# A hybrid decoder layer on one core: the conv state's share moved into FFN 1, ten taps per tile made by TensorE with diagonal matrices

## The chip, the core and the metric

The kernel runs on one NeuronCore of one Trainium2 chip. The metric is the device time of one execution in microseconds, the median of three runs. An execution uses five engines with a queue each: TensorE (PE; PEld are its weight loads), VectorE (DVE), ScalarE (ACT), GpSimd (POOL) and SyncE (SP), which issues the DMAs. Each engine works its own list of instructions strictly in order and waits where a semaphore tells it to.

## What is computed

One layer: half an FFN, a mixer, half an FFN. There are 256 prompt tokens and 64 decoded ones (8 sequences of 8), so T = 320 columns everywhere. The model width is 2048, an FFN 5632. The mixer has 16 attention heads and, beside them, 1024 channels of a convolution over time, 31 taps wide, each channel for itself:

```python
a, b = jnp.split(c, 2, axis=-1)
u = a * jax.nn.sigmoid(b)
...
u_ext = jnp.pad(u, ((0, 0), (CONV_STATE, 0), (0, 0)))                    # prompt: zeros ahead
conv = conv_branch(u_ext, dw_w, dw_b, ln_g, ln_b)
...
u_ext = jnp.concatenate([state_conv[l].astype(u.dtype), u], axis=1)      # decoded: 30 old values ahead
conv = conv_branch(u_ext, dw_w, dw_b, ln_g, ln_b)
...
def conv_branch(u_ext, dw_w, dw_b, ln_g, ln_b):
    y = lax.conv_general_dilated(u_ext, dw_w[:, None, :], window_strides=(1,), padding='VALID', ...)
    return jax.nn.silu(layernorm(y + dw_b, ln_g, ln_b))
```

For a decoded token the sum over 31 taps so falls into a share of the state, which is an input, and a share of the at most eight new values of its sequence. The layer norm goes over all 1024 channels. The attention of the decoded tokens reads a cache of 2048 positions (here called the sample work), that of the prompt tokens is small.

## The kernel before

**Layout.** Activations lie transposed, channels on the 128 partitions and T = 320 tokens along them: 16 tiles `yT` for the width, 8 tiles `cacc` for the conv's channels.

**Weights.** A weight piece is loaded by SP (`raw`), rounded by ACT to a high part `wh` (L243), and DVE makes the rest `wl` (L244); PE multiplies three times (L312 to L314: high by high, high by low, low by high) with 320 columns each. In FFN 1 and FFN 2 a piece is 4 x 128 rows by 256 columns, 24 products, and `wh` and `wl` have three buffers. In the mixer (`feed`, L743 and on) a piece is 2 x 128 by 256, 12 products; LA = 3 pieces are loaded ahead, LS = 1 piece is split ahead.

**The mixer's order.** First the q and k columns of w_in, then conv columns four times (`conv_in`: a gemm for a, one for b, two tiles each, 64 pieces in all), then the v columns four times (32 pieces), then W_out, its conv half first. After every piece `gemm` calls `tick()`, which runs what was put off with `defer(n, ...)`, and `after()`, which is `pump(na, nb)`: it advances the sample work by `na` steps, with a higher priority, and takes `nb` steps off a queue `bg` of background work. A scheduler then moves instructions within each engine by these priorities and an estimated timeline; what results is one fixed list for each engine.

**The sample work.** Per decoded sequence there are six far steps (POOL multiplies 128x1024 keys by the query, L569, DVE reduces them, L570; buffers `kf`, three of them), four near steps (keys are transposed by PE, `misc_kt` L593, and multiplied, `S` L600) and ten value steps (L659, L667).

**The convolution** (`conv_taps`). When a tile's b columns are there, `ev_b` loads its state (`state_in`: a DMA, two PE transposes, an ACT copy), POOL makes u (L844) and ACT copies it into a buffer of three, beside the state. Then `bg` gets the tile's steps. 21 taps are DVE's (L767 the first, L769). Ten taps (PTAPS) are ACT's and POOL's: ACT scales u (`cprod`, L774), POOL adds it up (`csum`, L778). Two steps `stap` make the decoded tokens: POOL multiplies 31-wide windows of state and new values by the taps (128x992, into a `kf` buffer, L787), DVE reduces them (L789). A last step adds `csum` (L802) and sums the tile for the norm. NBG = 5 steps go per piece. After the last conv tile come the 18 steps of the conv norm (`conv_norm`: mean, eight subtractions with squares, variance, eight scalings with SiLU). What is left in `bg` after the v columns runs at once.

Of the kernel before, what the change touches and what calls it, by code (L numbers as in the profile page):

```python
# [48 lines left out]
RATE_K = 0.55  # L49
RATE = 1.05  # L50
RATE_O = 1.6
NBG = 5
ORDER = "ccccvvvv"
MERGE = "fnffnfvnfvfvnvvvvvvv"
UW = ST + SEQ
UB = ST + TD
UTOT = UW + NB * UB
STG0, STGN = 16, 256


# [50 lines left out]
def block(ctx, tc, A, O):  # L111
# [105 lines left out]
    def tables():  # L217
# [81 lines left out]
    def gemm(feed, nk, hi, lo, evac, after=None, before=None):  # L299

        acc = [acc_tile() for _ in range(2)]
        for pc in range(nk // feed.nkp):
            if before:
                before(pc, feed)
            wh, wl = feed.get()
            for j in range(2):
                for k in range(feed.nkp):
                    kk = feed.nkp * pc + k
                    st, sp = kk == 0, kk == nk - 1
                    a = acc[j][:, 0:T]  # L310
                    h, l = wh[:, k, P * j:P * j + P], wl[:, k, P * j:P * j + P]
                    nc.tensor.matmul(a, h, hi[kk], start=st, stop=False)  # L312
                    nc.tensor.matmul(a, h, lo[kk], start=False, stop=False)  # L313
                    nc.tensor.matmul(a, l, hi[kk], start=False, stop=sp)  # L314
            tick()
            if after:
                after()
        for j in range(2):
            evac(j, acc[j][:, 0:T])

    class Ffn:
        def __init__(self, name, side=None):
# [104 lines left out]

        return f

    f1.run(W("ffn1_w_gate"), W("ffn1_w_up"), W("ffn1_w_down"), n1, lambda g: (nm.feed(g), nm.feed(g + 1)), x_chunks)  # L430


    mix = ExitStack()
# [315 lines left out]
    cprod = deque(cp.tile([P, 384], F32, name=f"cprod{i}", bufs=1) for i in range(3))
    csum = deque(cp.tile([P, 384], F32, name=f"csum{i}", bufs=1) for i in range(2))  # L750
    srow = deque(cp.tile([120, 2, P], F32, name=f"srow{i}", bufs=1) for i in range(2))
    ubuf = deque(cp.tile([P, UTOT], F32, name=f"u{i}", bufs=1) for i in range(3))
    for u in ubuf:
        nc.gpsimd.memset(u[:, 0:ST], 0.0)
    stf = A["state_conv"][0].rearrange("b t c -> (b t) c")
    ncp = O["new_conv_prompt"][0, 0]
    ncs = O["new_conv_sample"][0][:, ST - TD:ST, :]

    def conv_taps(i, u):
        a = cacc[i]  # L760
        ap, bias = a[:, 0:SEQ], gains[:, DWB + i:DWB + i + 1]
        s2 = {}

        def tap(j):
            w, src = dww[:, i, j:j + 1], u[:, j:j + SEQ]
            if j == 0:
                nc.vector.tensor_scalar(ap, src, w, bias, op0=ALU.mult, op1=ALU.add)  # L767
            else:
                nc.vector.scalar_tensor_tensor(ap, src, w, ap, op0=ALU.mult, op1=ALU.add)  # L769

        def ptap(j):
            first = "c" not in s2
            t = turn(csum if first else cprod)[:, 0:SEQ]
# [19 lines left out]
        nd = CW - PTAPS
        for j in range(nd):
            bg.append(lambda j=j: tap(j))
            k = (j + 1) * PTAPS // nd - j * PTAPS // nd
            for x in range(k):
                bg.append(lambda x=j * PTAPS // nd + x: ptap(nd + x))
            if j in (3, 9):
                bg.append(lambda j=j: stap(j > 3))  # L800
        def close():
# [15 lines left out]
    def state_in(i):  # L817
        sr = turn(srow)
        nc.sync.dma_start(sr, stf[:, P * i:P * i + P].rearrange("(r p) c -> p r c", p=120))
        m = mtile("st")  # L820
        for r in range(2):
            nc.tensor.transpose(m[:, 120 * r:120 * r + 120], sr[:, r, :], ident[0:120, 0:120])
        u = turn(ubuf)
        nc.scalar.copy(u[:, UW:UTOT].rearrange("p (b t) -> p b t", t=UB)[:, :, 0:ST],
                       m[:, 0:240].rearrange("p (b t) -> p b t", t=ST))
        return u

    def conv_in(g, after):
        at = {}
# [6 lines left out]
        def ev_b(j, ps):  # L836
            i = g + j
            t = wt("bt")
            nc.vector.tensor_tensor(t, ps, rstd, op=ALU.mult)
            nc.scalar.activation(t, t, AF.Sigmoid)  # L840
            u = state_in(i)
            us = u[:, UW:UTOT].rearrange("p (b t) -> p b t", t=UB)
            uc = at[j]
            nc.gpsimd.tensor_tensor(uc, at[j], t, op=ALU.mult)  # L844
            nc.scalar.copy(u[:, ST:UW], uc[:, 0:SEQ])
            nc.scalar.copy(us[:, :, ST:UB], uc[:, SEQ:T].rearrange("p (b t) -> p b t", t=TD))
            defer(6, lambda: u_out(i, uc))
            conv_taps(i, u)

# [222 lines left out]
```

## Time and profile before

| what | us |
|---|---|
| median of three runs | 2631.21 (2628.18 to 2635.72) |
| the profiled execution | 2634.91 |
| its span, first to last instruction | 2633.1 |
| PE busy | 2523.2 (96%) |
| DVE busy | 1458.9 (55%) |
| ACT busy | 1031.6 (39%) |
| POOL busy | 436.4 (17%) |

Busy shares are means over stages with different limits, so the slices of the span and windows of it are what to read. Times in the trace are counted from the span's start. A recorded matmul lasts longer than its turn in the array, since products are pipelined; PE's true rate is read from starts. PEclk is the share of the full clock (2.4 GHz) that TensorE was granted.

### The profile page before, as it was taken

To read this page: it belongs to the slowest core of one execution; us is meant where nothing else is said; L and a number is where in the kernel's file an instruction comes from. 1 tells how busy PE (TensorE), PEld (TensorE's weight loads), DVE (VectorE), ACT (ScalarE), POOL (GpSimd) and SP (SyncE) were. 2 spreads that over 40 slices of the span, in tenths; PEclk is the share of its full clock that TensorE was granted. 3 is DMA by queue.
4 is the path that set the end of the run, shared out by engine and by line. 5 is a ranking of instruction groups with operands and counts; after the bars stand their busy time and mean duration, and the time that the engine had idled before them with its cause. 6 is when DMAs were issued, how large, how long until landed. Compare 5 with 4: busy or idle time off the path is not lost.

```text
span 2633.1 us, 43093 instructions
## 1 busy us (share of the span) xinstructions
PE 2523.2 (96%) x17516; PEld 2411.1 (92%) x17516; DVE 1458.9 (55%) x1785; ACT 1031.6 (39%) x1605; POOL 436.4 (17%) x384
## 2 busy tenths in 40 slices
PE   8999999999999999798777899999999999999999
PEld 7999999999999999677666676999999999999999
DVE  5444444444444577969999744644444444444443
ACT  5332333233333456455443444533333333333333
POOL 2000000000000124737666300200000000000000
PEclk9999999999999999899988899999999999999999
DMA  7766767767667655776667756444444444444443
GB/s 221 214 205 212 205 214 208 210 212 203 213 216 199 203 158 180 219 220 211 223 217 250 235 178 212 133 150 152 147 150 153 148 149 152 149 148 152 151 148 119
DMA packets 486263, 489.60 MB, mean 186 GB/s; under 512 B 118250, under 2 KB 463266, under 8 KB 485280
## 3 DMA queue, kind: packets, MB, share of 16 engines
q1 hardware_dynamic: 486064, 486.84, 59.5%
q8 instruction: 137, 2.24, 0.4%
q14 instruction: 62, 0.51, 0.1%
HBM read 478.78 MB, written 59.04 MB: 204 GB/s over the span
## 4 chain that ended last, share of the span: by engine, by line
PE 41%; DVE 7%; issue 6%; DMA 2%; POOL 1%; ACT 1%; SPq 0%; ACTq 0%; DVEq 0%; POOLq 0%
PE acc L314 13%; PE acc L312 13%; PE acc L313 13%; DVE cacc L769 3%; DVE wl L244 2%; PE S L667 0%; DVE sf L570 0%; PE misc_kt L593 0%; DMA kf<-farK 0%; DMA raw<-w_out 0%; POOL kf L569 0%; PE S L600 0%; DVE cacc L892 0%; DVE cacc L767 0%; DMA kn<-cache_k 0%
## 5 line engine op out<-in xcount | busy, mean ns | idle before, releaser
L244 DVE TENSOR_TENSOR wl<-raw,wh 128x1024 fp32r<-128x1024 f32 (+1 forms) x736 | 871.6, 1186 | 923.4 <-ACT wh L243 920.1
L243 ACT CAST wh<-raw 128x1024 fp32r<-128x1024 f32 (+1 forms) x736 | 687.7, 936 | 1252.5 <-PE acc L313 1110.4
L314 PE MATMUL acc<-xh_a,wl 128*128 128x320 f32 x1408 | 436.1, 310 | 0.0
L313 PE MATMUL acc<-xl_a,wh 128*128 128x320 f32 x1408 | 436.1, 310 | 0.0
L312 PE MATMUL acc<-xh_a,wh 128*128 128x320 f32 x1408 | 435.5, 310 | 0.2 <-ACT wh L243 0.2
L314 PE MATMUL acc<-hh,wl 128*128 128x320 f32 x1408 | 435.5, 309 | 0.0
L312 PE MATMUL acc<-xh_c,wh 128*128 128x320 f32 x1408 | 435.3, 309 | 0.0
L314 PE MATMUL acc<-xh_c,wl 128*128 128x320 f32 x1408 | 435.1, 309 | 0.0
L313 PE MATMUL acc<-xl_c,wh 128*128 128x320 f32 x1408 | 435.1, 309 | 0.0
L313 PE MATMUL acc<-hl,wh 128*128 128x320 f32 x1408 | 435.0, 309 | 0.0
L312 PE MATMUL acc<-hh,wh 128*128 128x320 f32 x1408 | 435.0, 309 | 0.0
L368 POOL TENSOR_TENSOR hm<-ut,sg 128x320 f32<-128x320 f32 x88 | 78.4, 891 | 1652.9 <-DVE ut L366 1652.0
L314 PE MATMUL acc<-xh_b,wl 128*128 128x320 f32 x640 | 208.2, 341 | 67.1 <-DVE wl L244 66.9
L312 PEld LDWEIGHTS acc<-xh_a,wh 128*128 128x128 f32 x1408 | 264.8, 188 | 1.1 <-ACT wh L243 0.6
L314 PEld LDWEIGHTS acc<-xh_a,wl 128*128 128x128 f32 x1408 | 264.9, 188 | 0.5 <-issue 0.2
L313 PEld LDWEIGHTS acc<-xl_a,wh 128*128 128x128 f32 x1408 | 265.0, 188 | 0.3
L313 PEld LDWEIGHTS acc<-xl_c,wh 128*128 128x128 f32 x1408 | 264.3, 188 | 0.1
L312 PEld LDWEIGHTS acc<-xh_c,wh 128*128 128x128 f32 x1408 | 264.3, 188 | 0.1
L313 PEld LDWEIGHTS acc<-hl,wh 128*128 128x128 f32 x1408 | 264.3, 188 | 0.0
L314 PEld LDWEIGHTS acc<-hh,wl 128*128 128x128 f32 x1408 | 264.3, 188 | 0.0
L314 PEld LDWEIGHTS acc<-xh_c,wl 128*128 128x128 f32 x1408 | 264.3, 188 | 0.0
L312 PEld LDWEIGHTS acc<-hh,wh 128*128 128x128 f32 x1408 | 264.1, 188 | 0.0
(212 smaller groups left out, 2985.6 us busy)
## 6 DMA issues: line engine op xcount, KB each, us to landing
raw<-ffn_w_gate SPq DMA_DIRECT2D x176, 512.0 KB, 3.6
raw<-ffn_w_up SPq DMA_DIRECT2D x176, 512.0 KB, 3.8
raw<-ffn_w_down SPq DMA_DIRECT2D x176, 512.0 KB, 3.5
raw<-w_in SPq DMA_DIRECT2D x128, 256.0 KB, 4.1
farK<-cache_k SPq DMA_DIRECT2D x64, 384.0 KB, 4.8
farV<-cache_v SPq DMA_DIRECT2D x48, 512.0 KB, 4.8
kf<-farK SPq DMA_DIRECT2D x48, 512.0 KB, 4.6
vn<-farV SPq DMA_DIRECT2D x48, 512.0 KB, 5.7
```

Of the source, the lines that this page charges most:

```text
L243: nc.scalar.copy(dsth, src)
L244: nc.vector.tensor_tensor(dstl, src, dsth.bitcast(F32), op=ALU.subtract)
L312: nc.tensor.matmul(a, h, hi[kk], start=st, stop=False)
L313: nc.tensor.matmul(a, h, lo[kk], start=False, stop=False)
L314: nc.tensor.matmul(a, l, hi[kk], start=False, stop=sp)
L368: nc.gpsimd.tensor_tensor(m, t, sg[j], op=ALU.mult)
L769: nc.vector.scalar_tensor_tensor(ap, src, w, ap, op0=ALU.mult, op1=ALU.add)
```

## The change

- The state's share of the decoded tokens, with the bias, is made in FFN 1. `state_part` puts off one load per tile (`defer(40 + 20 * i)`), PE transposes, ACT copies the state into windows padded with zeros for the new values, and for each of 8 sequences DVE multiplies a 128x248 window by the taps and reduces it into `cold`. A table `wz` holds the taps that meet new values.
- In the mixer `stap` is one step: DVE multiplies the new values by `wz` (128x512), reduces, and adds `cold`.
- The ten ACT and POOL taps go. `diag` makes ten 128x128 diagonal matrices per tile on ACT, `dtaps` has PE multiply them with u in f32 and sum them in PSUM, and DVE's evacuation adds the bias. The 21 taps of DVE follow.
- u is written by POOL at its place at once, in one of five buffers; two ACT copies go. A tile may wait in the program for a buffer, by running `bg` steps.
- NBG is 2.6 steps per piece, with a carried rest.

```diff
-NBG = 5
+NBG = 2.6
...
+        for t in range(TD):
+            nc.gpsimd.tensor_copy(wz[:, :, t, 0:t + 1], dww[:, :, CW - 1 - t:CW])
...
+    def state_part(pool, win):
+        def load(i):
+            sr = pool.tile([120, 2, P], F32, name="srow", bufs=1)
+            nc.sync.dma_start(sr, stf[:, P * i:P * i + P].rearrange("(r p) c -> p r c", p=120))
+            defer(8, lambda: work(i, sr))
+
+        def work(i, sr):
+            m = mtile("st")
+            for r in range(2):
+                nc.tensor.transpose(m[:, 120 * r:120 * r + 120], sr[:, r, :], ident[0:120, 0:120])
+            o = win
+            nc.scalar.copy(o.rearrange("p (b t) -> p b t", t=UB)[:, :, 0:ST],
+                           m[:, 0:240].rearrange("p (b t) -> p b t", t=ST))
+            w = dww[:, i, :][:, None, :].to_broadcast([P, TD, CW])
+            for b in range(NB):
...
+                pr = pool.tile([P, TD, CW], F32, name="spr", bufs=1)
+                nc.vector.tensor_tensor(pr, x, w, op=ALU.mult)
+                nc.vector.tensor_reduce(cold[:, i, TD * b:TD * b + TD], pr, axis=mybir.AxisListType.X, op=ALU.add)
+            nc.scalar.activation(cold[:, i, :], cold[:, i, :], AF.Identity, bias=gains[:, DWB + i:DWB + i + 1])
+
+        for i in range(8):
+            defer(40 + 20 * i, lambda i=i: load(i))
...
     def bg_run(n):
-        while n > 0 and bg:
+        bgc[0] += n
+        while bgc[0] >= 1 and bg:
             bg.popleft()()
-            n -= 1
+            bgc[0] -= 1
...
+            for x in range(PTAPS // 2 * h, PTAPS // 2 * (h + 1)):
+                nc.scalar.activation(dg[0][:, x, :], ident, AF.Copy, bias=0.0, scale=dww[:, i, nd + x:nd + x + 1])
+
+        def dtaps():
+            m = mtile("dt")
+            for x in range(PTAPS):
+                nc.tensor.matmul(m[:, 0:SEQ], dg[0][:, x, :], u[:, nd + x:nd + x + SEQ], start=x == 0,
+                                 stop=x == PTAPS - 1)
+            nc.vector.tensor_scalar(ap, m[:, 0:SEQ], bias, None, op0=ALU.add)
...
-            nc.scalar.activation(t, u[:, j:j + SEQ], AF.Copy, bias=0.0, scale=dww[:, i, j:j + 1])
...
-                nc.gpsimd.tensor_tensor(s2["c"], s2["c"], t, op=ALU.add)
...
-            nc.gpsimd.tensor_tensor(pr4, win, w, op=ALU.mult)
...
-            nc.vector.tensor_reduce(d, pr.rearrange("p (b j) -> p b j", j=CW), axis=mybir.AxisListType.X, op=ALU.add)
...
+            nc.vector.tensor_tensor(pr, x, wz[:, i, :, :][:, None, :, :].to_broadcast([P, NB, TD, TD]), op=ALU.mult)
...
+            nc.vector.tensor_reduce(d, pr.rearrange("p b t s -> p (b t) s"), axis=mybir.AxisListType.X, op=ALU.add)
+            nc.vector.tensor_tensor(d, d, cold[:, i, :], op=ALU.add)
+
+        bg.extend([lambda: diag(0), lambda: diag(1), stap, dtaps])
+        bg.extend([lambda j=j: tap(j) for j in range(nd)])
+        bg.append(lambda: (norm_add("m", a, i), ran.append(i)))
...
-            nc.gpsimd.tensor_tensor(ap, ap, s2["c"], op=ALU.add)
...
+            while len(ran) < i - len(ubuf) + 1:
+                bg.popleft()()
+            u = turn(ubuf)
+            uc = u[:, ST:UT]
             nc.gpsimd.tensor_tensor(uc, at[j], t, op=ALU.mult)
-            nc.scalar.copy(u[:, ST:UW], uc[:, 0:SEQ])
```

Three places show how the lists of the engines change. The first is DVE in FFN 1, in a pair of gate and up columns; `gt` and `ut` are the evacuations. Before:

```order
L244 TENSOR_TENSOR wl<-raw,wh 128x1024 x3
L359 TENSOR_TENSOR gt<-acc,rstd 128x320 x2
L244 TENSOR_TENSOR wl<-raw,wh 128x1024 x4
L366 TENSOR_TENSOR ut<-acc,rstd 128x320 x2
L244 TENSOR_TENSOR wl<-raw,wh 128x1024
```

After, where the last conv tile's state is worked off:

```order
L391 TENSOR_TENSOR gt<-acc,rstd 128x320 x2
L248 TENSOR_TENSOR wl<-raw,wh 128x1024
L346 TENSOR_TENSOR spr<-win,dww 128x248
L347 TENSOR_REDUCE cold<-spr 128x8
...
L346 TENSOR_TENSOR spr<-win,dww 128x248
L248 TENSOR_TENSOR wl<-raw,wh 128x1024
L347 TENSOR_REDUCE cold<-spr 128x8
```

Two to three pairs of product and reduction now stand between two `wl`, eight pairs for a tile, eight tiles.

The second is DVE among the conv columns of the mixer, where a tile's taps begin. Before (tiles 9338 and 9339 are the fifth and the sixth):

```order
L767 TENSOR_SCALAR cacc_9338<-u_11053,dww,gains 128x256
L769 SCALAR_TENSOR_TENSOR cacc_9338<-u_11053,dww,cacc_9338 128x256 x4
L244 TENSOR_TENSOR wl<-raw,wh 128x512
L767 TENSOR_SCALAR cacc_9339<-u_11051,dww,gains 128x256
L769 SCALAR_TENSOR_TENSOR cacc_9338<-u_11053,dww,cacc_9338 128x256
L769 SCALAR_TENSOR_TENSOR cacc_9339<-u_11051,dww,cacc_9339 128x256
L244 TENSOR_TENSOR wl<-raw,wh 128x512
```

After (9601 is the third tile, 9602 the fourth, `nm` the norm's sum, `sf` a far step's reduction):

```order
L878 TENSOR_TENSOR nm_12265<-nm_12265,cacc_9601 128x320
L606 TENSOR_REDUCE sf<-kf 128x16
L655 RECIPROCAL st<-st 128x1
L816 TENSOR_SCALAR cacc_9602<-misc_dt,gains 128x256
L819 SCALAR_TENSOR_TENSOR cacc_9602<-u_11313,dww,cacc_9602 128x256
L606 TENSOR_REDUCE sf<-kf 128x16
L819 SCALAR_TENSOR_TENSOR cacc_9602<-u_11313,dww,cacc_9602 128x256 x2
L606 TENSOR_REDUCE sf<-kf 128x16
L819 SCALAR_TENSOR_TENSOR cacc_9602<-u_11313,dww,cacc_9602 128x256
L248 TENSOR_TENSOR wl<-raw,wh 128x512
```

Two tiles' taps were interleaved; now one tile is done after the other, and each begins with an evacuation of PE's sum `misc_dt`.

The third is PE around the mean of the conv norm (`misc_mu`). Before, among v columns (`xh_b`, `xl_b`):

```order
L312 MATMUL acc<-xh_b_9153,wh 128x320
L313 MATMUL acc<-xl_b_9154,wh 128x320
L868 MATMUL misc_mu<-nm_11916,onesC 128x320
L659 MATMUL misc_pt<-ident,px 128x128 x4
L314 MATMUL acc<-xh_b_9153,wl 128x320
```

After, with the last v transposes (`misc_vo`) ahead and the first conv product of W_out (`ch`) at the end:

```order
L922 MATMUL misc_vo<-ident,w_9622 128x128 x2
L923 MATMUL misc_vo<-ident,w_9622 64x128
L883 MATMUL misc_mu<-nm_12265,onesC 128x320
L883 MATMUL misc_mu<-nm_12652,onesC 128x320
L883 MATMUL misc_mu<-nv_14963,onesC 128x320
L695 MATMUL misc_pt<-ident,px 128x128 x4
L667 MATMUL misc_pl<-vS,ptz 32x256 x4
L883 MATMUL misc_mu<-nv_14968,onesC 128x320
L703 MATMUL S<-vn,pt 32x256 x12
...
L316 MATMUL acc<-ch_15017,wh 128x320 x2
```

The mean and the variance moved from the middle of the v columns to behind them, with a few value blocks of the sample work between them and W_out.

## Rows read from the trace of the kernel before

**Rows 1.** The page's 40 slices of the span, busy tenths, and clock tenths

```profile
PE   8999999999999999798777899999999999999999
DVE  5444444444444577969999744644444444444443
PEclk9999999999999999899988899999999999999999
```

**Rows 2.** Busy time by stretch: FFN 1, the mixer's stage, W_out

```profile
core 0: us, PE busy (x) PEld busy (x) DVE busy (x) ACT busy (x) POOL busy (x), PEclk, DMA share, GB/s
300.00:900.00 600.00, 600.00 (x4093) 600.00 (x4093) 269.53 (x294) 203.13 (x230) 26.69 (x31) 1.00 0.70 210
1118.60:1482.00 363.40, 294.81 (x2305) 242.77 (x2304) 334.86 (x402) 181.12 (x404) 216.49 (x170) 0.91 0.69 226
1482.00:1640.00 158.00, 148.03 (x1136) 106.50 (x1136) 76.53 (x226) 62.64 (x168) 9.09 (x8) 0.96 0.59 195
```

**Rows 3.** Waits from 1118 to 1482: who, for whom, us, times, longest

```profile
PE acc L314 <- DVE wl L244: 54.9, 32, 5.0
```

**Rows 4.** DVE's groups, 1118 to 1482: busy us, mean ns, idle before

```profile
L769 DVE SCALAR_TENSOR_TENSOR cacc<-u,dww,cacc 128x256 f32<-128x256 f32 x160 | 137.4, 890 | 0.5
L244 DVE TENSOR_TENSOR wl<-raw,wh 128x512 fp32r<-128x512 f32 x94 | 96.0, 1025 | 16.6 <-ACT wh L243 16.6
L570 DVE TENSOR_REDUCE sf<-kf 128x16 f32<-128x1024 f32 x29 | 34.9, 1205 | 0.0
L789 DVE TENSOR_REDUCE cacc<-kf 128x32 f32<-128x992 f32 x16 | 18.8, 1174 | 0.0
L892 DVE TENSOR_TENSOR cacc<-cacc,mu 128x320 f32<-128x320 f32 x4 | 7.1, 1804 | 0.0
L767 DVE TENSOR_SCALAR cacc<-u,dww,gains 128x256 f32<-128x256 f32 x8 | 7.0, 880 | 4.5 <-ACT u L845 4.5
L879 DVE TENSOR_TENSOR cacc<-cacc,mu 128x320 f32<-128x320 f32 x8 | 7.0, 945 | 0.8 <-ACT mu L876 0.8
```

**Rows 5.** POOL's groups, 1118 to 1482

```profile
L569 POOL TENSOR_TENSOR kf<-kf,qr 128x1024 f32<-128x1024 f32 x28 | 71.4, 2552 | 24.0 <-DMA kf<-farK 16.6 <-DVE cacc L769 6.4 <-DVE st L619 1.0
L778 POOL TENSOR_TENSOR csum<-csum,cprod 128x256 f32<-128x256 f32 x72 | 65.0, 906 | 12.1 <-ACT cprod L774 9.1
L787 POOL TENSOR_TENSOR kf<-u,dww 128x992 f32<-128x992 f32 x16 | 38.6, 2420 | 14.7 <-DVE cacc L789 6.5 <-ACT u L824 5.3 <-DVE sf L570 2.7
...
L802 POOL TENSOR_TENSOR cacc<-cacc,csum 128x256 f32<-128x256 f32 x8 | 8.0, 1002 | 18.2 <-DVE cacc L769 18.2
```

**Rows 6.** DVE's timeline: start us, length of the run us, instruction, count

```profile
1209.38 3.60 DVE L769 SCALAR_TENSOR_TENSOR cacc<-u,dww,cacc 128x256 f32<-128x256 f32 x4
1212.90 1.22 DVE L244 TENSOR_TENSOR wl<-raw,wh 128x512 fp32r<-128x512 f32 x1
1214.05 4.92 DVE L769 SCALAR_TENSOR_TENSOR cacc<-u,dww,cacc 128x256 f32<-128x256 f32 x11
1218.89 0.68 DVE L244 TENSOR_TENSOR wl<-raw,wh 128x512 fp32r<-128x512 f32 x1
```

**Rows 7.** PE's timeline: one f32 product with 320 columns (two records)

```profile
1454.14 0.70 PE L868 MATMUL misc_mu<-nv,onesC 128*128 128x320 f32 x2
1454.68 0.38 PE L907 MATMUL misc_vo<-ident,w 128*128 128x128 f32 x2
```

**Rows 8.** PE's value products, 1118 to 1482 (eight records a block)

```profile
L667 PE MATMUL S<-vn,pt 128*32 128x256 f32 x400 | 34.7, 416 | 3.1 <-DMA vn<-farV 2.8 <-ACT pt L553 0.3
```

**Rows 9.** Timeline of the conv norm: mean, reciprocal, first W_out product

```profile
1434.92 0.81 PE L868 MATMUL misc_mu<-nm,onesC 128*128 128x320 f32 x2
...
1458.04 2.15 DVE L889 RECIPROCAL mu<-sd 128x320 f32<-128x320 f32 x1 [1.47 <-ACT sd L887]
...
1481.86 0.39 PE L312 MATMUL acc<-ch,wh 128*128 128x320 f32 x1
```

**Rows 10.** DVE's groups, 300 to 900: the weights' rest in FFN 1

```profile
L244 DVE TENSOR_TENSOR wl<-raw,wh 128x1024 fp32r<-128x1024 f32 x171 | 216.5, 1266 | 288.0 <-ACT wh L243 288.0
```

More of the change, by code (lines that the diff above doesn't have):

```diff
@@ L51 @@
 RATE_O = 1.6
-NBG = 5
+NBG = 2.6
 ORDER = "ccccvvvv"
 MERGE = "fnffnfvnfvfvnvvvvvvv"
-UW = ST + SEQ
+UT = ST + T
 UB = ST + TD
-UTOT = UW + NB * UB
 STG0, STGN = 16, 256
@@ L141, in block @@
     dww = const.tile([P, 8, CW], F32, name="dww")
+    wz = const.tile([P, 8, TD, TD], F32, name="wz")
+    nc.gpsimd.memset(wz, 0.0)
+    cold = const.tile([P, 8, TS], F32, name="cold")
     G1, GM, G2, DWB, LNG, LNB, QN, KN = 0, 16, 32, 48, 56, 64, 72, 73
@@ L428, in x_chunks @@
         return f
-    f1.run(W("ffn1_w_gate"), W("ffn1_w_up"), W("ffn1_w_down"), n1, lambda g: (nm.feed(g), nm.feed(g + 1)), x_chunks)
+    with tc.tile_pool(name="stp", bufs=1) as stp:
+        win = stp.tile([P, NB * UB], F32, name="win")
+        nc.gpsimd.memset(win, 0.0)
+        state_part(stp, win)
+        f1.run(W("ffn1_w_gate"), W("ffn1_w_up"), W("ffn1_w_down"), n1, lambda g: (nm.feed(g), nm.feed(g + 1)), x_chunks)
     mix = ExitStack()
@@ L705, in block @@
     bg = deque()
+    bgc = [0.0]
     def bg_run(n):
-        while n > 0 and bg:
+        bgc[0] += n
+        while bgc[0] >= 1 and bg:
             bg.popleft()()
-            n -= 1
+            bgc[0] -= 1
+        if not bg:
+            bgc[0] = 0.0
     smp = sample()
@@ L748, in block @@
     cp = cst.enter_context(tc.tile_pool(name="cp", bufs=2))
[L749 to L752, printed above, removed]
+    ubuf = deque(cp.tile([P, UT], F32, name=f"u{i}", bufs=1) for i in range(5))
     for u in ubuf:
         nc.gpsimd.memset(u[:, 0:ST], 0.0)
-    stf = A["state_conv"][0].rearrange("b t c -> (b t) c")
     ncp = O["new_conv_prompt"][0, 0]
     ncs = O["new_conv_sample"][0][:, ST - TD:ST, :]
+    ran = []
     def conv_taps(i, u):
@@ L761, in conv_taps @@
         ap, bias = a[:, 0:SEQ], gains[:, DWB + i:DWB + i + 1]
-        s2 = {}
-        def tap(j):
[L765 to L773, printed above, removed]
-            nc.scalar.activation(t, u[:, j:j + SEQ], AF.Copy, bias=0.0, scale=dww[:, i, j:j + 1])
-            if first:
-                s2["c"] = t
-            else:
-                nc.gpsimd.tensor_tensor(s2["c"], s2["c"], t, op=ALU.add)
@@ L793, in conv_taps @@
[L793 to L801, printed above, removed]
-            nc.gpsimd.tensor_tensor(ap, ap, s2["c"], op=ALU.add)
-            norm_add("m", a, i)
-        bg.append(close)
+        nd = CW - PTAPS
@@ new lines, in conv_taps, with diag @@
+        dg = []
+        def diag(h):
+            if not dg:
+                dg.append(cp.tile([P, PTAPS, P], F32, name="diag"))
+            for x in range(PTAPS // 2 * h, PTAPS // 2 * (h + 1)):
[6 more added lines that the diff above has]
+            nc.vector.tensor_scalar(ap, m[:, 0:SEQ], bias, None, op0=ALU.add)
@@ new lines, in tap, with stap @@
+        def tap(j):
+            nc.vector.scalar_tensor_tensor(ap, u[:, j:j + SEQ], dww[:, i, j:j + 1], ap, op0=ALU.mult, op1=ALU.add)
+        def stap():
+            pr = cp.tile([P, NB, TD, TD], F32, name="cpr", bufs=1)
+            x = u[:, ST + SEQ:UT].rearrange("p (b s) -> p b s", b=NB)[:, :, None, :].to_broadcast([P, NB, TD, TD])
+            nc.vector.tensor_tensor(pr, x, wz[:, i, :, :][:, None, :, :].to_broadcast([P, NB, TD, TD]), op=ALU.mult)
+            d = a[:, SEQ:T]
+            nc.vector.tensor_reduce(d, pr.rearrange("p b t s -> p (b t) s"), axis=mybir.AxisListType.X, op=ALU.add)
+            nc.vector.tensor_tensor(d, d, cold[:, i, :], op=ALU.add)
@@ L815, in u_out @@
         nc.sync.dma_start(ncs[:, :, P * i:P * i + P], uo[0:TS, 1, :])
[L817 to L826, printed above, removed]
     def conv_in(g, after):
```

16 lines of the change are left out of this document (3 added, 13 removed).

## The prediction

> **What bounds the kernel now.** I read the page's slices first [rows 1]. TensorE (PE) is at 9 tenths nearly everywhere, except in slices 15 to 22, the mixer. There VectorE (DVE) climbs to 9 and PE's granted clock drops from full. The busy times by stretch [rows 2] say the same in numbers. In FFN 1 (300 to 900 us) PE is busy 600 of 600 us and DVE 270. From the end of the k columns to the first W_out product (1118.6 to 1482, which I call the stage: 363.4 us for the conv and v columns) DVE is busy 334.9 us, PE 294.8 at a clock of 0.91. After it (1482 to 1640) PE is busy 148 of 158 us, and DVE has half its time free. So FFN 1 and FFN 2 are PE's, the stage is DVE's. The waits confirm it [rows 3]: PE stood 54.9 us before the third product of a weight piece, 32 times, until DVE had made `wl`. The code makes only one piece ahead (LS = 1), so every tap that DVE has queued before the next `wl` is time for PE too.
>
> Why is DVE so long in it? Its groups [rows 4]: 160 taps of 890 ns, 137.4 us, and 94 `wl` of 1025 ns, 96.0 us. Neither needs that long. At 1214 us eleven taps take 4.92 us together, 0.45 each, and the `wl` behind them 0.68; 5 us earlier four taps take 3.60, 0.90 each, and the `wl` next to them 1.22 [rows 6]. What differs is GpSimd (POOL): in the stage it is busy 216.5 us [rows 2] with products of two tensors [rows 5]. The reductions, with one input, last 1174 to 1205 ns on the whole stage [rows 4], so they are not slowed. The Trainium skill, "SBUF — State Buffer", section "Who interferes with whom", gives the rule: a VectorE instruction with two SBUF inputs and a GpSimd instruction that reads SBUF exclude each other for a whole instruction. The trace agrees: 0.45 against 0.90 us, and reductions that don't change.
>
> **The change, part by part.** I make the sum against the profiled run (2634.91 us, span 2633.1; median of the runs 2631.21) and apply the difference to the median.
>
> *POOL work that goes.* 72 additions of `csum` (65.0 us), 16 state products (38.6) and 8 closing additions (8.0) [rows 5] make 111.6 us, 52% of POOL's 216.5. DVE's time lost to POOL is 160 x (0.89 - 0.45) = 70 us in taps and 94 x (1.025 - 0.64) = 36 in `wl` (0.64: the recorded 0.68 less some of the 0.08 by which records overlap, as the eleven taps' end at 1218.97 and the `wl` behind them show [rows 6]). Of these 106 I give back 52%: 55 us. Below lies 40, if the far multiplications (28 of 2552 ns [rows 5]) hold DVE more once POOL is free for them; above 106. By the page's rule alone, each of the 111.6 us could be 1 us of DVE back, and DVE's sum below would be 198 and not 255.
>
> *DVE instructions.* Gone: 16 state reductions, 18.8 us [rows 4]. Each tile had 1 + 20 taps and now has 21 taps and one evacuation of the diagonal products, some 0.45 more, which the contended first taps (7.0 us for 8 [rows 4]) pay for: 0. New: for each of 8 tiles a product over 512 elements (0.64, like a `wl`), a reduction over 512 (1.17 x 512/992 = 0.6) and a small addition (0.2): 11.5. In the order of after, 32 far reductions stand between the last k column and W_out, where the trace of before has 29 [rows 4]: 3 x (1.2 + 1.6) = 8. DVE: 334.9 - 55 - 18.8 + 11.5 + 8 = 281. Of it about 26 (subtractions and scalings of the conv norm, 7.0 + 7.1 [rows 4], with their additions, splits and the reciprocal) now stands behind all v columns. That leaves **DVE 255 us** for conv and v columns.
>
> *PE.* Ten products with a diagonal in f32, 128x256, for each of 8 tiles: the nearest row is the mean's product, f32, 320 columns, 0.54 us until the next starts [rows 7]. By columns 0.43, x 80 = 34 us. The bound above: if each of its two weight loads were not hidden, 30 us more. The 16 state transposes go to FFN 1: -2. In the order of after, PE has also done 8 more value blocks and 2 more key blocks at the first W_out product. 50 value blocks (400 records) took 34.7 us [rows 8], so 8 take 5.6; I count 6 in all, and take 6 off behind the stage, where PE is the bound. What PE does now is 294.8 us at clock 0.91 [rows 2], or 268 at full clock. **PE: 268 + 34 - 2 + 6 = 306 us**, more than DVE's 255. So the bound changes engines, and conv and v columns take 306. Here the clock decides. In FFN 1, where PE never stops, the clock is 1.00; in the stage, where it waits for `wl`, 0.91 [rows 2], a mix of the levels 1.2 and 2.4 GHz. The Trainium skill, "TensorE: Matmul & The Clock Gate", section "What's actually happening", says that an idle array gets the slow clock and a busy one the full. By that rule 306; with the clock of now 295 + 34 - 2 + 6 = 333. FFN 1 agrees, so I take 306.
>
> *The conv norm.* NBG goes from 5 to 2.6 per weight piece while a tile still has 26 background steps (34 before). 8 x 26 + 18 are 226 steps, 80 pieces x 2.6 only 208: the 18 of the norm run after the last v column. The order says so too: PE's mean product stands behind the last v transposes. Now the norm takes from 1434.92 (second mean product) to 1481.86 (first W_out product) [rows 9], but PE has v columns and DVE other work in between. Alone it is two mean products (1.1), 8 subtractions (3.6 at 0.45), squares and sums on ACT, POOL and DVE (3), two variance products (1.1), root and its table (2), the reciprocal (2.15 [rows 9]), scaling, SiLU and split of the first tile (2), with copies and signals: some 18 us. PE finds only a few value blocks in it, and then the tiles arrive slower than it eats them. I charge **+18** (bounds 8, and 47, the length now).
>
> *FFN 1.* 64 pairs of product and reduction over 248 elements go onto DVE: 0.45 + 0.35 (estimates from the tap and from 1.17 x 248/992), 51 us in all. Three pairs between two `wl` are 2.4 + 1.27 = 3.7 us; a weight piece costs PE 24 x 600/4093 = 3.5 [rows 2]. DVE sat idle 288 us before its 171 `wl` [rows 10], and pieces are three buffers deep, so a burst of two pieces is hidden. If that cover were gone: 51 us. PE pays for the 16 transposes, 2. Eight small loads on the SP queue stand among pieces that it issues ahead. I charge **+4** (2 to 12): 2 for the transposes, 2 for what bursts leave.
>
> *The sum.* Stage 363 -> 306 + 18 = 324: -39. Behind it -6. FFN 1 +4. Total -41: 2594 for the profiled run, **2590** for the median.
>
> **Rivals.**
>
> *The engines alternate.* An evacuation of the diagonal products stands in DVE's order with less than a piece of `wl` made ahead, so DVE waits there for PE, and then PE for the `wl` that stands some ten rows further on: 8 x 4.3 us of products that overlap nothing, or PE stays at 0.91. Conv and v columns 333 to 340: 2617 to 2624. For it: the one-piece lead, and PE's 32 waits now [rows 3]. Against: PE has key and value blocks in between.
>
> *PE has more room than its rows tell.* A weight product lasts 0.31 us in its record and the next starts after 0.15, so every burst ends with time that isn't needed. Then conv and v columns take about 280, near DVE's 255: 2564.
>
> *Weight loads of the diagonals aren't hidden:* +30, 2620. Against: the mean's two passes follow each other in 0.54 us, loads included [rows 7].
>
> *Slower: DVE's new work in FFN 1 is not hidden.* All 64 pairs delay `wl` and with it PE. If half of the products meet POOL's `hm` as taps meet `csum`, a pair is 0.68 + 0.35, 64 of them 66 us in place of the 2 charged for bursts' rest: 2654. It decides once DVE's lead over PE is under one burst's excess over its pieces, some 2 x 1 us. Against: 288 idle us before `wl` [rows 10], PE without a pause there, POOL busy only 27 of 600 us [rows 2].
>
> **How the numbers follow.** Forecast 0.55 (2575 to 2612), more room 0.17, alternation 0.17, loads 0.04, FFN 1 not hidden 0.07. From the first three comes the range, 2558 to 2626; it leaves out little more than FFN 1. A measurement tells 0.3%, 7.9 us: faster is below 2623.3, slower above 2639.1. Faster: 0.55 + 0.17 + half of alternation and of loads = 0.82; same 0.11; slower 0.07.
>
> **What the profile after would show.** Taps near 0.6 us in place of 0.89 and `wl` near 0.8; PE over 90% busy from the k columns to the mean product at a clock near 1, its wait for `wl` well under 30 us; 160 records of diagonal products with 0.21 us spacing; a gap of 10 to 18 us in PE after the last v column; in FFN 1 no wait of PE for `wl`. I would be wrong if taps kept their 0.89, if PE's wait for `wl` stayed (alternation), or if FFN 1 grew by over 10 us.

## The result, and the profile after

The changed kernel takes **2600.97 us** (median, 2596.43 to 2607.19); the kernel before took 2633.14 beside it. The ratio is 0.9882, 95% interval 0.9851 to 0.9912: 32 us faster, where 41 were forecast. The profiled execution (2597.02, near the low end of its runs) has a span of 2595.2 us against 2633.1, so the traces show 37.9 us of difference.

The page's slices of after, to be read against [rows 1]: DVE's nines went from five to two, PE's sevens in slices 19 to 21 (counted from 0) are nines, and the clock has one eight left. Slice 17 (1103 to 1168 us, the end of the k columns and the first conv columns) fell from nine to seven.

```profile
PE   8999999999999999879999899999999999999999
DVE  5445555555544477987897646644444444444443
PEclk9999999999999999899999999999999999999999
```

For the mixer I cut the windows at DVE's last evacuation of the k, of the conv and of the v columns, and at the first product of each half of W_out. Columns as in [rows 2]. Before (conv columns, v columns, W_out's conv half):

```profile
1118.70:1350.60 231.90, 192.35 (x1550) 159.37 (x1548) 207.46 (x262) 120.53 (x266) 132.22 (x112) 0.93 0.66 215
1350.60:1480.60 130.00, 100.97 (x737) 82.30 (x737) 125.90 (x141) 59.18 (x136) 82.87 (x58) 0.87 0.73 244
1481.90:1633.80 151.90, 141.93 (x1101) 101.45 (x1099) 73.00 (x216) 57.87 (x156) 9.19 (x8) 0.96 0.58 191
```

After (FFN 1, conv columns, v columns, the gap up to W_out, its conv half):

```profile
300.00:900.00 600.00, 600.00 (x4096) 599.97 (x4095) 305.10 (x390) 206.74 (x242) 26.39 (x30) 1.00 0.69 211
1119.80:1351.90 232.10, 210.67 (x1696) 174.17 (x1695) 187.18 (x268) 109.86 (x253) 90.71 (x58) 0.96 0.80 263
1351.90:1449.60 97.70, 97.39 (x825) 85.89 (x823) 72.09 (x134) 42.40 (x98) 15.28 (x13) 1.00 0.73 239
1449.60:1471.10 21.50, 12.26 (x81) 5.88 (x81) 13.92 (x22) 12.71 (x26) 7.51 (x8) 0.76 0.55 182
1471.10:1595.90 124.80, 123.86 (x944) 91.95 (x944) 64.53 (x212) 57.75 (x154) 3.32 (x4) 1.00 0.52 175
```

The surprise is in the lengths. The conv columns, where 82 of the 111.6 us of removed POOL work had stood, are as long as before: 232.1 and 231.9. The v columns lose 32.3 us, the gap costs 20.2 more, and W_out's conv half loses 27.1. What follows lasts 999.3 us in both.

A second reading makes this comparable, and I use it for every kernel below. Busy time of PE times its granted clock is PE's **work at full clock**; what the window has beyond that is **lost** (PE waits, or runs slowly). It is an estimate, since the granted clock is the mean of a window and has two digits: a hundredth of it is 2 us in the conv columns. From the last k evacuation to W_out's second half:

| kernel | conv | v | gap | W_out conv half | work | lost |
|---|---|---|---|---|---|---|
| before | 231.9 | 130.0 | 1.3 | 151.9 | 404 | 111 |
| after | 232.1 | 97.7 | 21.5 | 124.8 | 433 | 43 |

The work grows by 29 us, about what the diagonal products cost, and 68 us of loss go. Of the 43 that are left, 30 lie in the conv columns (232.1 - 210.67 x 0.96) and 12 in the gap. So the conv columns' equal length is a sum of two changes: work rose there from 179 (192.35 x 0.93) to 202 us, and loss fell from 53 to 30.

Why are 30 us still lost in the conv columns? DVE's groups there, after, and then the three of before that answer to them:

```profile
L819 DVE SCALAR_TENSOR_TENSOR cacc<-u,dww,cacc 128x256 f32<-128x256 f32 x105 | 63.6, 605 | 2.0
L248 DVE TENSOR_TENSOR wl<-raw,wh 128x512 fp32r<-128x512 f32 x64 | 63.1, 993 | 18.4 <-ACT wh L247 17.9 <-PE acc L318 0.4
L606 DVE TENSOR_REDUCE sf<-kf 128x16 f32<-128x1024 f32 x26 | 30.9, 1209 | 6.5 <-POOL kf L605 6.1 <-ACT S L612 0.3
```

```profile
L769 DVE SCALAR_TENSOR_TENSOR cacc<-u,dww,cacc 128x256 f32<-128x256 f32 x118 | 97.1, 856 | 0.4
L244 DVE TENSOR_TENSOR wl<-raw,wh 128x512 fp32r<-128x512 f32 x64 | 60.4, 947 | 16.6 <-ACT wh L243 16.6
L570 DVE TENSOR_REDUCE sf<-kf 128x16 f32<-128x1024 f32 x13 | 15.7, 1207 | 0.0
```

Taps are faster, but `wl` is not, and the far reductions have doubled. POOL's far multiplications tell why, after and before:

```profile
L605 POOL TENSOR_TENSOR kf<-kf,qr 128x1024 f32<-128x1024 f32 x27 | 68.2, 2541 | 80.7 <-DMA kf<-farK 55.9 <-DVE cacc L819 24.5 <-DVE st L653 0.2
```

```profile
L569 POOL TENSOR_TENSOR kf<-kf,qr 128x1024 f32<-128x1024 f32 x12 | 30.0, 2500 | 17.0 <-DMA kf<-farK 9.5 <-DVE cacc L769 6.4 <-DVE st L619 1.0
```

15 far steps that stood further back moved into the conv columns, now that POOL is freer and the state products no longer share the `kf` buffers (e4 below bears on the buffers). What one such product does to DVE and PE is seen in the timelines of POOL, DVE and PE at 1211 us (start, length of the run, count):

```profile
1211.12 2.39 POOL L605 TENSOR_TENSOR kf<-kf,qr 128x1024 f32<-128x1024 f32 x1 [1.68 <-DMA kf<-farK]
1213.44 0.20 POOL L657 MEMSET z<- 128x120 f32 x1
1213.60 5.19 POOL L605 TENSOR_TENSOR kf<-kf,qr 128x1024 f32<-128x1024 f32 x2
```

```profile
1211.28 2.78 DVE L248 TENSOR_TENSOR wl<-raw,wh 128x512 fp32r<-128x512 f32 x1
1213.98 2.61 DVE L819 SCALAR_TENSOR_TENSOR cacc<-u,dww,cacc 128x256 f32<-128x256 f32 x1
1216.51 2.82 DVE L248 TENSOR_TENSOR wl<-raw,wh 128x512 fp32r<-128x512 f32 x1
1219.26 0.99 DVE L819 SCALAR_TENSOR_TENSOR cacc<-u,dww,cacc 128x256 f32<-128x256 f32 x2
1220.17 0.69 DVE L248 TENSOR_TENSOR wl<-raw,wh 128x512 fp32r<-128x512 f32 x1
```

```profile
1219.39 0.42 PE L318 MATMUL acc<-xh_b,wl 128*128 128x320 f32 x1 [3.40 <-DVE wl L248]
```

Three products in a row let exactly one two-input instruction of DVE through each. A `wl` of 0.69 us takes 2.8, two of them come late together, and PE stands 3.40 us. PE's wait for `wl` in the conv columns is made of six places:

```profile
PE acc L318 <- DVE wl L248: 12.0, 6, 3.4
```

At each of them a two-input instruction of DVE, the `wl` itself or one shortly ahead of it, ran beside a far product and lasted 1.44 to 2.82 us. The rest of the 30 us is smaller waits (9 us) and the clock of 0.96 (8 us).

### The profile page after: what moved, and what is told of

Its sections match the earlier page's. It is cut to its first block, busy times and chain, and to the rows that moved or that the text cites. A ratio compares the mean times of both kernels' runs of the same rounds, so it can differ in the third digit from the quotient of the medians.

```text
span 2595.2 us, 43398 instructions
## 1 busy us (share of the span) xinstructions
PE 2532.7 (98%) x17676; PEld 2427.0 (94%) x17676; DVE 1436.4 (55%) x1929; ACT 1020.4 (39%) x1589; POOL 329.0 (13%) x300
## 4 chain that ended last, share of the span: by engine, by line
PE 50%; DVE 3%; DMA 2%; issue 1%; POOL 1%; ACT 0%; SPq 0%; ACTq 0%; DVEq 0%; POOLq 0%
PE acc L317 15%; PE acc L316 15%; PE acc L318 15%; PE S L703 1%; DVE wl L248 1%; PE misc_dt L814 1%; DMA kf<-farK 1%; PE misc_kt L629 1%; DVE sf L606 1%; DMA vn<-farV 1%; DVE cacc L819 1%; PE S L636 1%; POOL kf L605 0%; PE misc_pt L695 0%; PE misc_ps L973 0%
## 5 line engine op out<-in xcount | busy, mean ns | idle before, releaser
L248 DVE TENSOR_TENSOR wl<-raw,wh 128x1024 fp32r<-128x1024 f32 (+1 forms) x736 | 858.0, 1168 | 888.5 <-ACT wh L247 881.6
L318 PE MATMUL acc<-xh_b,wl 128*128 128x320 f32 x640 | 201.3, 326 | 24.6 <-DVE wl L248 24.5
```

What stands on the lines that cost most here:

```text
L248: nc.vector.tensor_tensor(dstl, src, dsth.bitcast(F32), op=ALU.subtract)
```

## The experiments

My theory after this comparison: PE's work is what it is, the loss in the conv columns comes from far steps that POOL now does there, in bursts that delay `wl`; the gap and W_out's gain belong together, since sample work moved from behind to the front. Rivals: the diagonal sums or the one-piece lead make PE and DVE alternate; the diagonal products are a cost that cancels what they give.

**The two halves of the change.** In `e1_state_only` the taps stay with ACT and POOL (the five u buffers and the small `stap` are kept):

```
-NBG = 2.6
+NBG = 5
...
-        bg.extend([lambda: diag(0), lambda: diag(1), stap, dtaps])
...
+            for x in range(k):
+                bg.append(lambda x=j * PTAPS // nd + x: ptap(nd + x))
+            if j == 3:
+                bg.append(stap)
```

> The state's share is made in FFN 1 and `stap` is the small one on DVE, but the ten taps per tile stay with ACT and POOL (no diagonal products; five steps per piece as before). Theory (the gain is DVE time given back by POOL, and the two halves add up): POOL loses 38.6 us of state products, DVE wins 34 of blocked time and 18.8 - 11.5 of instructions, about 40 us of DVE in a stage that DVE bounds, less what far steps drawn forward take back; 2610 to 2620 against 2633 before, taps still near 0.8 us. Rival (the diagonal products are only a cost for PE, 34 us, and the state's half is the whole gain): 2595 to 2603, at or under the changed kernel.

Measured: **2597.98**, ratio 0.9864 (0.9848 to 0.9880). The theory fell, the rival's range holds: the state's half alone is as fast as the whole change.

In `e2_diag_only` the state stays in the mixer:

```
-        state_part(stp, win)
...
+            state_in(i, u)
...
-        bg.extend([lambda: diag(0), lambda: diag(1), stap, dtaps])
+        bg.extend([lambda: diag(0), lambda: diag(1), lambda: stap(0), dtaps, lambda: stap(1)])
```

> The ten taps per tile become diagonal products (2.6 steps per piece, as in the changed kernel), but the state is loaded and multiplied in the mixer as before: 16 POOL products of 2.4 us in kf buffers. Theory (halves add up): POOL loses 73 us of csum additions and closings, PE gets 34 us of products; 2612 to 2622 against 2633 before. Rival (diagonal products cost PE what they give DVE): 2630 to 2640, no gain.

Measured: 2624.68, ratio 0.9962 (0.9949 to 0.9976), between the two ranges. So -35 and -8 by themselves, -32 together: in the changed kernel the halves don't add up.

| kernel | conv | v | gap | W_out conv half | work | lost |
|---|---|---|---|---|---|---|
| e1 | 224.1 | 106.6 | none | 147.1 | 403 | 75 |
| e2 | 228.9 | 120.2 | 29.1 | 130.8 | 434 | 75 |

Each half alone removes 36 us of loss. But the diagonals bring 30 us of work with them, so for them little is left. (In e2 a tile has one step more at the same 2.6 per piece, and four u buffers where the changed kernel has five, so part of its gap is its own.)

**The norm's place.** `e3_nbg34` changes one number:

```
-NBG = 2.6
+NBG = 3.4
```

> The changed kernel with 3.4 background steps per weight piece instead of 2.6: the conv norm's mean stands before 128 of the v columns' 384 high products and not behind them. Theory (the 22.1 us from the last v product to the first W_out product is exposed latency of the norm, and DVE has room in the v columns, 73 busy of 98): the gap falls to 2 to 6 us, v columns grow by up to 8, total 10 to 18 us less than the changed kernel, 2583 to 2591. Rival (DVE's 26 us of norm fill the v columns, and PE waits there for wl instead): no change within 5 us, 2596 to 2606.

Measured: **2590.01**, ratio 0.9836 (0.9822 to 0.9851), 11 us under the changed kernel; theory. But not in the way that I wrote it. The v columns did not grow, and W_out did (conv columns, v columns, W_out):

```profile
1117.70:1353.30 235.60, 213.31 (x1709) 177.18 (x1707) 192.14 (x285) 112.17 (x263) 88.43 (x58) 0.95 0.77 257
1353.30:1451.30 98.00, 94.03 (x756) 82.57 (x755) 83.17 (x139) 52.48 (x114) 23.78 (x21) 0.98 0.69 219
1451.30:1591.90 140.60, 138.72 (x1088) 98.34 (x1081) 65.03 (x211) 55.88 (x152) 3.33 (x4) 1.00 0.61 200
```

In the gap of after PE had done sample work (12.26 us busy), which now stands in W_out. What the gap cost was its loss of 12 us, not its length of 21.5.

e3 also bears on the halves. In e1 too the norm's mean stands among the v columns, and about as many far reductions stand in the conv columns (25, in e3 26). From e1 to e3 the work rises by 31 us and the loss falls by 34 (the table under e12 has e3): with the norm there the diagonal products were worth 8 us. The changed kernel, with its gap, did not show them. Against e3's 43 us the halves' 35 and 8 do add up, in part by chance, as e2 has a gap of its own.

**The far steps' place.** `e4_kfshare` lets the state product take a `kf` buffer again:

```
-            pr = cp.tile([P, NB, TD, TD], F32, name="cpr", bufs=1)
+            pr = sa.tile([P, AW], F32, name="kf", bufs=3)[:, 0:NB * TD * TD].rearrange("p (b t s) -> p b t s", b=NB, t=TD)
```

> The changed kernel with the new small state product in a `kf` buffer again, so that it takes turns with the far steps as before: at the end of the conv columns the list of DVE holds 36 of 48 far reductions and not 42. Theory (far steps drawn into the conv columns ate the gain there: each costs DVE 1.2 us of reduction and 1.1 to 1.6 of blocked time): conv columns 218 to 224 us instead of 232, v columns longer by 6 to 14, total within 6 us of the changed kernel. Rival (PE and the one-piece lead set the conv columns): conv columns stay at 229 to 235, total the same.

Measured: 2605.12, ratio 0.9893 (0.9879 to 0.9908). Conv columns 223.6 (theory), v columns 114.9 (17 longer, 3 more than I gave). The length is the theory's, its reason is not shown: PE's work in the conv columns fell from 202 to 195 us and the loss there stayed at 29, while the v columns now lose 15. Sample work changed its stretch, with its time.

**Far products off POOL.** `e5_no_far_product`:

```
-            nc.gpsimd.tensor_tensor(k3, k3, qr[:, None, :].to_broadcast([P, 16, HD]), op=ALU.mult)
```

> The changed kernel with POOL's far multiplications left out (48 products of 128x1024; DVE reduces the raw keys, so the decoded tokens' attention leaves the query out of the far scores). Theory (the conv columns stay long because POOL's far products, 27 of them there, hold DVE's two-input instructions, 31 us by overlap): taps fall to 0.47 us, conv columns from 232 to 208 to 216 us, v columns stay at 98, total 2577 to 2587. Rival (DVE's lost time is not what PE waits for; the one-piece lead and the diagonal sums set the conv columns): conv columns 226 to 234, total 2593 to 2603.

Measured: 2560.88, ratio 0.9718 (0.9702 to 0.9735). Conv columns 209.2: theory. The total is 40 us lower, 16 beyond the range, since the q and k columns, which I had not counted, gained 15 (last k evacuation at 1104.9 instead of 1119.8). Only 4.5 us are lost in the conv columns, where the changed kernel loses 30. The conv columns, and DVE's two groups there:

```profile
1104.90:1314.10 209.20, 204.69 (x1739) 171.18 (x1737) 148.96 (x260) 111.73 (x259) 20.83 (x31) 1.00 0.84 281
```

```profile
L818 DVE SCALAR_TENSOR_TENSOR cacc<-u,dww,cacc 128x256 f32<-128x256 f32 x100 | 49.4, 494 | 2.0
L248 DVE TENSOR_TENSOR wl<-raw,wh 128x512 fp32r<-128x512 f32 x65 | 45.8, 710 | 23.6 <-ACT wh L247 15.7 <-PE acc L318 4.4 <-ACT pt L589 2.6
```

**The diagonal products.** `e6_one_diag`:

```
-            for x in range(PTAPS):
+            for x in (0,):
```

> The changed kernel with one diagonal product per tile instead of ten (72 of 80 f32 products and nine taps per tile left out; the diagonals are still made). Theory A (PE's length bounds conv and v columns, 72 products of 0.43 us): 31 us shorter in all, 2566 to 2574. Theory B (the conv columns alternate, and PE only waits longer there): 10 to 18 us shorter, 2583 to 2591, the gain in the v columns and with a longer wait for wl. Rival C (the products are hidden altogether): 2596 to 2604.

Measured: 2577.84, ratio 0.9784 (0.9765 to 0.9804): 23 us for 72 products, between A and B. The work fell by 31 us to 402, the loss grew to 57. They are not hidden; in the total, three quarters of them count. Where the gain stands can't be read from this run: the conv columns fell to 203.1 us, but with 69 taps in them instead of 105, and the gap grew to 37.1.

**The lead.** `e7_two_ahead`:

```
-LA, LS = 3, 1
+LA, LS = 3, 2
```

> The changed kernel with two weight pieces split ahead in the mixer instead of one (LS = 2; three buffers as before). Theory (PE and DVE alternate because DVE is one piece ahead): PE's wait for wl falls from 24.6 to under 8 us, conv columns from 232 to 215 to 224, total 2583 to 2593. Rival (the waits are DVE's length or the far steps', not the lead): conv columns 228 to 236, total 2596 to 2606.

Measured: 2603.36, ratio 0.9877 (0.9855 to 0.9900), conv columns 236.3: the rival. In the whole mixer PE waited 21.7 us for `wl`, where it had waited 24.5 in the changed kernel; the theory had it under 8. Another piece ahead in the list gives nothing where `wl` itself is late.

**FFN 1.** `e8_no_state`:

```
+                if b == 0:
                     pr = pool.tile([P, TD, CW], F32, name="spr", bufs=1)
...
+                else:
+                    nc.scalar.copy(cold[:, i, TD * b:TD * b + TD], o[:, UB * b:UB * b + TD])
```

> The changed kernel with FFN 1's state products and reductions made for one of eight sequences (the other seven get a copy by ACT, so the decoded tokens' convolution lacks their state). Theory (the pairs are hidden behind PE in FFN 1, but for bursts): 0 to 4 us shorter, 2597 to 2602. Rival (they delay wl): 8 to 15 us shorter, 2585 to 2593.

Measured: 2605.86, ratio 0.9884 (0.9863 to 0.9906), the changed kernel's own. The state's work in FFN 1 costs nothing that can be measured. By the second reading e8 has 429 us of work and 52 lost, where the changed kernel, with the same code in the mixer, has 433 and 43. So in those columns differences under some 9 us tell nothing.

**A version without the bursts.** `e9_far_on_dve`, on top of e3:

```
-            nc.gpsimd.tensor_tensor(k3, k3, qr[:, None, :].to_broadcast([P, 16, HD]), op=ALU.mult)
+            nc.vector.tensor_tensor(k3, k3, qr[:, None, :].to_broadcast([P, 16, HD]), op=ALU.mult)
```

> As e3 (3.4 steps per piece), with the far multiplications on DVE in place of POOL: 48 products of 128x1024 that should last about 1.2 us each. Theory (a POOL product of 2.55 us costs DVE about as much time as doing the product itself, 31 us / 27 = 1.15 us each): conv columns within 5 us of e3's 235.6; q and k columns some us shorter; total 2580 to 2592. Rival (the lock costs more than its overlap shows, as e5 gained 40 us in all): conv columns 215 to 225, total 2568 to 2578. Third (DVE becomes the bound): 2595 or more.

Measured: **2573.06**, ratio 0.9770 (0.9756 to 0.9785), 17 us under e3: the conv columns and the total lie in the rival's ranges, though the theory's premise on DVE's time held. The conv columns, DVE's groups in them, and PE's wait there for `wl` in e3 and then in e9:

```profile
1118.80:1339.20 220.40, 213.49 (x1758) 178.02 (x1757) 186.08 (x311) 116.37 (x272) 24.17 (x32) 0.98 0.82 279
```

```profile
L819 DVE SCALAR_TENSOR_TENSOR cacc<-u,dww,cacc 128x256 f32<-128x256 f32 x120 | 54.0, 484 | 0.5
L248 DVE TENSOR_TENSOR wl<-raw,wh 128x512 fp32r<-128x512 f32 x63 | 44.2, 710 | 14.6 <-ACT wh L247 14.2 <-issue 0.3
L605 DVE TENSOR_TENSOR kf<-kf,qr 128x1024 f32<-128x1024 f32 x26 | 31.5, 1212 | 7.9 <-DMA kf<-farK 7.8
```

```profile
PE acc L318 <- DVE wl L248: 18.4, 7, 5.8
```

```profile
PE acc L318 <- DVE wl L248: 1.4, 2, 0.7
```

This is the run that decides for the conv columns. DVE's busy time, blocked time included, hardly changed there (192.1 to 186.1 us, with 31.5 us of products taken on), yet PE's wait for `wl` went from 18.4 to 1.4. In them it was not DVE's sum that PE waited for. It was up to 2.8 us at a time, when POOL held up one or more instructions of DVE just ahead of a `wl`.

In the q and k columns the same move gave nothing: the last k evacuation is at 1118.8 us, in e3 at 1117.7, where the expectation had some us less. At their end (1080 to 1104.9) DVE is busy without a pause in both runs (e3, e9; columns as in [rows 2]):

```profile
1080.00:1104.90 24.90, 21.09 (x128) 19.32 (x128) 24.90 (x22) 11.80 (x27) 17.59 (x10) 0.86 0.79 232
1080.00:1104.90 24.90, 19.90 (x118) 18.03 (x111) 24.90 (x28) 9.15 (x21) 6.25 (x6) 0.86 0.72 217
```

So there DVE had no room, which fits that moving the products gave nothing and that leaving them out (e5) gave 15 us.

**Slower sample work.** `e10_slow_sample`, on top of e3:

```
-            conv_in(g, pump(RATE, NBG))
+            conv_in(g, pump(0.6, NBG))
-RATE_O = 1.6
+RATE_O = 2.8
```

> As e3, with the sample work advanced by 0.6 steps per piece in the conv columns instead of 1.05, and by 2.8 instead of 1.6 behind the v columns: 36 far reductions stand before the last conv product and not 42, and PE does a quarter less sample work by W_out. Theory (the conv columns are long because sample work is crowded into them, and PE does it at full rate behind): conv columns 210 to 222, W_out's first half longer by the moved work, total 2578 to 2588. Rival (the work only moves, PE's sum stays): within 5 us of e3, 2585 to 2595.

Measured: 2609.75, ratio 0.9908 (0.9893 to 0.9923), 20 us worse than e3; both theories missed. The conv columns did shrink, to 209.7, but W_out grew by 48. The v columns and W_out's conv half:

```profile
1328.80:1421.60 92.80, 88.76 (x717) 78.68 (x717) 80.20 (x128) 47.06 (x98) 30.32 (x21) 1.00 0.73 236
1421.60:1609.80 188.20, 171.16 (x1401) 117.25 (x1401) 80.83 (x232) 73.71 (x194) 14.92 (x13) 0.93 0.66 220
```

The work is e3's (433 us), the loss 58 instead of 41: in W_out 29 us are lost to a clock of 0.93 and to waits, the largest group of them for the loads of value rows (11.9 us, 10 times). Sample work that was moved behind the v columns, at 2.8 steps per piece, cost more there than in the conv columns.

**Fewer diagonals.** `e11_eight_taps` (on e3) and `e12_far_dve_eight` (on e9):

```
-PTAPS = 10
+PTAPS = 8
```

> As e3, with eight diagonal products per tile instead of ten: 16 products fewer on PE (6.9 us at 0.43) and 16 taps more on DVE (8 to 11 us). Theory (DVE and PE are both nearly full in the conv columns, so a tap's place is worth little): within 6 us of e3, 2584 to 2596. Rival (PE bounds): 2580 to 2584. Second rival (DVE bounds): 2597 to 2602.

> As e9 (3.4 steps per piece, far multiplications on DVE), with eight diagonal products per tile instead of ten. Theory (with POOL out of the way PE bounds the conv and v columns: it was busy 213.5 of 220.4 and 87.4 of 88.7 us in e9): 16 products of 0.43 us less, 4 to 9 us shorter than e9, 2564 to 2569. Rival (16 more taps of 0.48 us fill DVE, and the norm's mean moves back, from 128 high products ahead of the last v product to 59): a gap before W_out, 2573 to 2584.

Measured: 2586.38, ratio 0.9823 (0.9807 to 0.9840), and **2569.07**, ratio 0.9756 (0.9739 to 0.9773), each 4 us under its base. This says little, as each interval meets that of its base. In e12 theory and rival were both at work: PE's conv and v columns took 14 us less than in e9, and a gap of 16.9 us opened as the mean moved back. It is the fastest kernel here that computes the whole layer (e5 leaves a product out), 32 us under the changed one.

| kernel | conv | v | gap | W_out conv half | work | lost |
|---|---|---|---|---|---|---|
| e3 | 235.6 | 98.0 | none | 140.6 | 434 | 41 |
| e5 | 209.2 | 94.4 | 21.6 | 129.5 | 431 | 23 |
| e9 | 220.4 | 88.7 | none | 141.7 | 434 | 17 |
| e12 | 213.5 | 81.5 | 16.9 | 135.3 | 428 | 19 |

## Why the prediction was right in its total, and where not

The total was 9 us off as a difference (32 us against 41) and inside the range. Two of its steps were off by more than that, the conv and v columns by 24 us too short and the part behind by 21 too long. That they nearly cancelled is luck.

- **PE's sum: right.** 306 us were forecast for conv and v columns; PE was busy 210.67 + 97.39 = 308 there, 300 at full clock. The price of the diagonals was right: 0.216 us from record to record over 16 in a row, 34.5 for all 160 (forecast 34). PE's timeline shows 16 of them, until the next group starts:

```profile
1198.94 3.62 PE L814 MATMUL misc_dt<-u,diag 128*128 128x256 f32 x16
1202.39 1.04 PE L629 MATMUL misc_kt<-ident,kn 128*128 128x128 f32 x8
```

- **DVE's sum: right.** 255 forecast, 187.18 + 72.09 = 259 measured. Taps were 0.56 and `wl` 0.91 in the whole stage, where 0.6 and 0.8 were named. With the free lengths of the prediction (0.45 and 0.64), DVE's time lost to POOL fell from 106 to 45 us: some 61 given back, where I took 55. The far steps had been counted over the whole stage (3 more), and what I missed is that 13 more changed places in it.

```profile
L819 DVE SCALAR_TENSOR_TENSOR cacc<-u,dww,cacc 128x256 f32<-128x256 f32 x168 | 94.2, 561 | 3.4
L248 DVE TENSOR_TENSOR wl<-raw,wh 128x512 fp32r<-128x512 f32 x97 | 87.7, 909 | 29.7 <-ACT wh L247 26.9 <-DMA vn<-farV 2.0 <-PE acc L318 0.4
```

- **"More than DVE's 255, so the columns take 306": the step that failed.** They took 329.8. A sum over a stage of two unlike parts hides that in the first part both engines are crowded (PE 202 at full clock and DVE 187 of 232), and that DVE's work comes in lumps. The conv columns lost 30 us, the v columns none. The lower bound that I gave for POOL's share (40 us, if the far multiplications hold DVE more) named the cause, but I took it for a matter of DVE's sum. The six waits above and e9 show that in the conv columns it is one of bursts.
- **The conv norm: right as a length, too dear as a charge.** +18 forecast, +20.2 measured; but PE did sample work in it, and e3, with the norm among the v columns, was 11 us faster and not 18. Its timeline, against [rows 9]:

```profile
1449.99 1.24 PE L883 MATMUL misc_mu<-nm,onesC 128*128 128x320 f32 x4
1464.19 2.15 DVE L904 RECIPROCAL mu<-sd 128x320 f32<-128x320 f32 x1 [1.41 <-ACT sd L902]
1471.14 0.54 PE L316 MATMUL acc<-ch,wh 128*128 128x320 f32 x2
```

- **Behind the stage: mis-sized.** Forecast -6, measured -27.1. PE's work there fell by 12 (141.93 x 0.96 = 136 to 124); the loss fell by 15 (from 15.6 to 0.9), of which I had counted nothing, though [rows 2] shows the 0.96 and the 10 us without work. The longest wait there had been one of 5.7 us for `wl`; after, PE waits 0.9 us in all. Some us of this come and go: in e8, which differs from the changed kernel in FFN 1 alone, the same half took 128.1 us at a clock of 0.97, against 124.8 at 1.00.

```profile
PE acc L314 <- DVE wl L244: 5.7, 1, 5.7
PE S L703 <- DMA vn<-farV: 0.9, 1, 0.9
```

- **FFN 1: right** (+4 forecast, about 0 by e8; the k columns end 1.1 us later). DVE's idle time before `wl` fell from 288 [rows 10] to 254.7 us; the pairs last 0.42 and 0.41.

```profile
L248 DVE TENSOR_TENSOR wl<-raw,wh 128x1024 fp32r<-128x1024 f32 x171 | 216.3, 1265 | 254.7 <-ACT wh L247 254.1
L346 DVE TENSOR_TENSOR spr<-win,dww 128x248 f32<-128x248 f32 x48 | 19.9, 415 | 1.1
L347 DVE TENSOR_REDUCE cold<-spr 128x8 f32<-128x248 f32 x48 | 19.6, 408 | 1.0
```

- **The rivals.** Alternation left its sign (DVE waited for the diagonal sums, 13.9 us in five of eight), but a second piece ahead changed nothing (e7), and with the far products off POOL the loss fell from 41 to 17 us (e9). More room, unhidden weight loads and a slower FFN 1 did not come. Of the signs named, `wl` (0.91 us for 0.8) and the gap (21.5 us for 10 to 18) missed.

Not settled: how much of the 36 us of loss that each half removes alone is the same loss. e1 and e3 suggest little of it; for an answer e2 would have to run without its gap and with the far steps in e3's places. Not run either: e1 with the far products on DVE, which would tell whether the diagonal products are worth their 29 us of work once POOL is out of the way.

## What to carry to other kernels

Count a stage as work of the bounding engine at full clock plus what it loses, for each stretch between two changes of load. A change that takes work off one engine can let its queue run ahead, so look at which instructions move up into the crowd. A long instruction of a side engine that locks out another one has two prices: where the locked engine has room, the delay that it puts in front of a consumer (the conv columns in e9), and where it has none, its share of that engine's time (as the end of the k columns suggests).

## What the runs showed of the hardware

- The far product of 128x1024 lasts 2.54 us on POOL and 1.21 on DVE. In the conv columns DVE's busy time is about the same whether it does the products itself (186.1 us, e9) or is locked out by POOL's (192.1, e3). The Trainium skill, "GPSIMD Engine Reference", section "4.1 Engine selection", says that products of two tensors belong on VectorE and are about twice as slow on GpSimd; 2.54 to 1.21 agrees, and e9's 17 us are what following it was worth here.
- The lock is whole instructions long, as the Trainium skill, "SBUF — State Buffer", section "Who interferes with whom", has it: a `wl` that started 0.16 us after a POOL product lasted 2.78 us instead of 0.69. That POOL products in a row let one DVE instruction through each is what the timeline at 1211 us adds.
- By that section's rule alone each us of POOL's removed 111.6 could have been one of DVE's. By the means of taps and `wl` about 61 came back.
